# One chain of eight heads in place of two chains of four in the RWKV-7 recurrence of a hybrid layer

## The chip, the cores and the metric

The kernel runs on one core of a Trainium2 chip. The metric is the device time of one execution in microseconds; of several runs the median is given. Below, TensorE is the matmul engine, VectorE, ScalarE and GpSimd are the elementwise engines, SyncE issues most DMA transfers and GpSimd some of the stores. PSUM is the memory into which matmuls write, in eight banks of 512 fp32 columns per partition.

## The reference

One trunk layer over 1152 tokens (1024 latent, 128 context), width 1024, all in fp32. A normalised and modulated input is projected once; four heads of an HGRN2 gated recurrence and eight heads of RWKV-7 time mixing, each in both directions, work on the result; an output projection and a gated ConvFFN follow. The part that the change concerns is RWKV-7:

```python
def rwkv7_scan(r, w, k, v, kk, a, s0):
    ...
    def step(S, inp):
        r_t, w_t, k_t, v_t, kk_t, a_t = inp
        sk = jnp.einsum('bhij,bhj->bhi', S, kk_t)
        S = (S * w_t[:, :, None, :] - sk[..., None] * (kk_t * a_t)[:, :, None, :]
             + v_t[..., None] * k_t[:, :, None, :])
        return S, jnp.einsum('bhij,bhj->bhi', S, r_t)
```

Eight heads of 64 and two directions make sixteen independent states of 64 x 64. The outputs of both directions are added, normalised per head and gated. Context scans start from zero, latent scans from cached states.

## The kernel before, in words

The scan is done in chunks of 64 tokens, 18 chunks (16 of the latents, 2 of the context), in the order `ORDER = [*range(10), 16, 17, *range(10, 16)]`. Forward and backward run side by side: in step n the forward scan takes chunk n and the backward scan chunk 15 - n. A pair p of heads (h = 0, 1 in partitions 0 to 63 and 64 to 127) in direction d is one column block w of 64. Four pairs by two directions are eight blocks; the kernel splits them into two groups g of four blocks, and `chains(0)` and `chains(1)` are two generators that are advanced in turn.

Before the recurrence, `features` works out the decayed operands of each pair and stores them to DRAM: `kr` (L1484) and, from `elim`, the inverted 64 x 64 systems (L1549 to L1565) to `d_ak`, `kb` (L1487, L1489) to `d_kb`, and the values, transposed to tokens by rows, to `d_v` (L1423, one store of 128 columns for each direction and stretch of chunks). One step of one group then does this:

- `load_step` loads `kb` (L1757) and the operand array W, for each h (L1759); `load_values` loads the 64 value rows into half of X (L1766) and copies them into its second slot (L1767). W and X have one buffer for each group.
- `prep`: matmuls of kb and W (L1776), two masked evictions by VectorE for each h (L1781 into W, L1783), four transposes of kb (L1790) and their eviction (L1791).
- R1: eight matmuls of W with X (L1820) into the PSUM tile R, copied to r1 (L1822). R2: eight with r1 (L1827) into R, copied into X for each h (L1829).
- State: L1835 and L1837 into R, multiplied by the chunk's decay into X for each h (L1854). Output: L1846 and L1848 into the PSUM tile Y, copied to yt for each direction (L1872), and stored to `d_y` after every second step (L1875).

Each fp32 matmul shows as two records in the trace. PSUM tiles of the two groups share banks:

```python
plan.tag("r", [(mp, 2048), (mp, 2304)], 256)
plan.tag("y", [(mp, 2560), (mp, 2816)], 256)
```

Bank 4 begins at column 2048 of `mp`, bank 5 at 2560. The tag `a` (banks 2, 3, 6, 7) serves `prep`, the hgrn blocks and the adaLN matmuls.

Other work stands around the recurrence: projections of the HGRN2 inputs (`proj`, L1125 to L1127, matmuls of 128 x 128 by 384 columns), `hgrn_block` with many matmuls of 32 columns (L1646 and others), `hgrn_out`, `ada_block`, and in the end `wo_tile`, the output projection, whose tiles need finished outputs. After that come the ConvFFN (L2120) and its down projection (L2269 to L2271).

The order is not written by hand. Every call is recorded as an operation; a planner (`Plan.schedule`) gives each a cost and simulates the engines, taking at each moment the ready operation with the highest rank: the length of the work that hangs on it, plus a lead for its kind (`LEADS`), plus a nudge for each sixteen operations (`NUDGE`), with penalties for a change of matmul shape on TensorE. Each engine then runs its list in that order. Copies may go to ScalarE or VectorE, stores to SyncE's or GpSimd's queue, as the planner finds them free. Operations inside `plan.together()` stay together.

Of the kernel before, what the change touches and what calls it, by code (L numbers as in the profile page):

```python
# [20 lines left out]
P = 128  # L21
# [25 lines left out]
BUSY = 168.59  # L47
NUDGE = {1: 6, 3: -7, 4: -41, 5: -2, 7: 9, 8: 9, 9: 9, 10: 9, 11: 20, 12: 19, 13: 19, 14: 15, 15: 15, 16: 5, 17: -4, 18: -1, 19: -4, 20: -18, 21: -29, 22: -19, 23: -26, 24: -26, 25: -6, 27: -3, 28: -3, 29: -3, 30: -3, 31: -5, 32: -3, 33: -3, 35: -3, 51: -5, 52: -5, 53: -2, 84: -6, 85: -6, 86: -6, 87: -6, 88: 6, 91: -3, 92: -6, 93: -6, 94: -6, 95: -6, 96: -6, 97: -6, 98: -6, 104: -7, 105: -4, 108: -6, 109: 4, 110: -6, 111: -6, 119: 6, 127: -7, 140: 6, 141: 6, 142: 6, 143: 21, 144: 6, 145: 6, 147: -2, 172: -17, 173: -17, 174: -17, 175: -17, 183: -14, 184: -20, 185: -4, 189: 57, 190: 57, 191: 69, 193: 5, 194: 3, 200: -15, 201: -8, 203: 11, 204: 14, 206: 3, 212: -16, 217: 13, 218: 5, 224: -48, 225: -15, 226: -15, 227: -15, 236: 7, 239: -2, 243: -26, 244: -26, 245: -26, 246: -19, 247: -26, 251: 7, 252: 7, 253: 5, 254: -12, 266: -4, 269: 3, 275: 61, 282: -16, 290: -9, 292: 2, 294: 18, 295: 18, 296: 18, 297: 28, 298: 28, 299: 28, 300: 48, 301: 48, 302: 30, 303: 27, 305: 30, 306: 30, 307: 30, 308: 37, 309: 40, 310: 40, 311: 40, 312: 51, 313: 42, 314: 47, 315: 43, 316: 23, 317: 26, 318: 26, 319: 23, 320: 23, 321: 23, 322: 23, 323: 22, 328: 10, 329: 13, 330: 29, 331: 29, 337: -10, 338: -10, 339: -10, 340: -10, 341: -10, 342: -10, 343: -10, 344: 10, 345: 10, 346: 5, 347: 8, 348: 8, 349: 8, 350: 11, 351: 8, 352: -12, 353: -14, 354: -8, 355: -14, 356: 15, 357: -2, 358: 33, 359: 7, 360: -4, 361: 4, 362: -3, 363: -4, 364: 7, 365: -7, 367: 13, 368: 23, 370: 25, 377: 6, 378: 13, 379: 13, 380: 18, 381: 18, 382: 18, 390: 1, 396: 6, 398: 5, 400: -10, 401: -10, 404: -6, 405: -6, 406: -6, 407: -6, 408: -6, 409: -6, 410: -6, 411: -6, 412: -6, 413: -2, 416: -23, 417: 3, 418: 3, 419: 3, 425: -3, 426: -3, 427: -3, 428: -3, 453: -3, 454: -3, 455: -5, 456: 20, 457: 5, 458: 20, 459: 3, 460: -15, 461: 1, 462: -4, 463: -11, 464: -4, 465: -4, 466: -4, 467: -4, 468: -4, 469: -2, 470: 32, 471: 15, 472: 15, 473: 16, 474: 1, 475: 1, 476: 15, 477: 10, 478: 14, 479: 15, 480: 28, 481: 10, 482: 12, 483: 34, 484: 24, 485: 26, 486: 6, 487: 21, 488: 6, 489: 11, 490: 20, 491: 13, 492: 25, 493: 2, 494: -16, 495: -5, 496: -5, 497: -5, 498: -5, 499: -43, 500: -20, 501: -18, 502: -16, 503: -39, 504: -13, 505: -12, 506: -12, 507: -15, 508: -36, 509: -37, 510: -24, 511: -24, 512: -38, 516: 21, 517: 22, 518: 22, 519: 11, 520: 11, 521: 11, 522: 1, 523: 11, 524: 1, 525: 11, 526: 9, 527: 26, 528: -1, 529: 1, 530: -5, 532: -34, 533: -34, 534: -26, 535: -27, 536: 8, 537: 22, 538: 22, 539: 45, 540: 16, 541: 18, 542: 14, 543: 14, 544: 4, 545: 13, 546: 4, 547: 4, 548: 53, 549: 39, 550: 39, 551: 52}
LEADS = {'ada_block': 46.4, 'bonus_rows': 27.8, 'chains': -35.7, 'const': 113.0, 'conv_rkv': 0.0, 'down_weights': -36.2, 'elim': -4.6, 'features': 0.0, 'ffn_down': 14.5, 'ffn_mid': -1.7, 'finish': 52.5, 'finish_last': -12.3, 'first_columns': -38.6, 'front': 0.0, 'gate_row': 0.0, 'hgrn_block': -3.6, 'hgrn_in': 0.0, 'hgrn_out': 113.5, 'late': -0.7, 'made': 3.5, 'mod_columns': -1.2, 'mod_scale': 70.4, 'modulated': -24.2, 'pair': 8.2, 'param_loads': 9.6, 'params': -96.8, 'post': 3.0, 'prep': 119.5, 'product': -3.4, 'put': 0.0, 'save': 4.8, 'step_kernel': -1.0, 'stored': 0.0, 'three': -10.1, 'total': -0.3, 'turned': 4.0, 'weights': 0.0, 'wo_tile': 5.1}
# [769 lines left out]
def step_kernel(ctx: ExitStack, tc: tile.TileContext, I, O):  # L819
# [52 lines left out]
    def banks(name, first, count, each=1, free=False):  # L872
# [26 lines left out]
    NW = 1  # L899
    Layout(low, 0, N0).add("W", 1536, 2 * NW).add("X", 512, 4).add("ckb", 512, 2).add("ar", 512, 2) \  # L900
        .add("ckt", 512, 2).add("r1", 256, 2).add("amask", 192)
    plan.tag("sv", [(low, 8896), (top, 0)], 256)

    Layout(top, 256, N1).add("yt", 512, 2).add("s_in", 512).add("hs", 2304).add("qyo", 768).add("sco", 384).add("vao", 384).add("g2", 384) \
# [51 lines left out]
    plan.tag("r", [(mp, 2048), (mp, 2304)], 256)  # L956
    plan.tag("y", [(mp, 2560), (mp, 2816)], 256)
# [192 lines left out]
    akr = [[dram(f"d_ak{g}", [P, 16, 4, 192]), dram(f"d_akp{g}", [P, 2, 4, 192])] for g in range(2)]  # L1150
    kbd = [dram(f"d_kb{g}", [P, NCH, 4, P]) for g in range(2)]

    vx = [dram(f"d_v{g}", [T, 512]) for g in range(2)]
# [17 lines left out]
    dcs = cst("dcs", [P, 2, NCH, 4])  # L1171
# [9 lines left out]
    def akr_at(g, n0, n):  # L1181

        return akr[g][0][:, n0:n0 + n] if n0 < 16 else akr[g][1][:, n0 - 16:n0 - 16 + n]
# [189 lines left out]
    def features(p, r, k, v):  # L1373
# [16 lines left out]
        for tb in range(3):  # L1390
# [18 lines left out]
            for d in range(2):  # L1409
# [10 lines left out]
                for ch, n0, n in steps_of(d, 6 * (2 - tb if d else tb), 6):  # L1420
                    at = (ch - 6 * (2 - tb if d else tb)) // 2
                    w0 = P * (2 * (p % 2) + d)
                    st(vx[p // 2][64 * n0:64 * (n0 + n), w0:w0 + P].rearrange("(a p) c -> p a c", p=P),  # L1423
                       vt.rearrange("p (a b) -> p a b", b=P)[:, at:at + n // 2, :])
# [4 lines left out]
            for d in range(2):  # L1429
                sg = tb if d == 0 else 2 - tb  # L1430
                c0 = 6 * sg
                w, g = 2 * (p % 2) + d, p // 2
# [16 lines left out]
                for ch, n0, n in steps_of(d, c0, 6):  # L1449
                    pool.tensor_copy(dcs[:, g, n0:n0 + n, w], dd[:, ch - c0:ch - c0 + n, 64])  # L1450
# [31 lines left out]
                for ch, n0, n in steps_of(d, c0, 6):  # L1482
                    sc_ = slice(ch - c0, ch - c0 + n)
                    st(akr_at(g, n0, n)[:, :, w, 0:128], kr[:, sc_, :])  # L1484

                    ko = kbd[g][:, n0:n0 + n, w, :]
# [8 lines left out]
    def elim(akd, ako, nu, name, tag):  # L1495
# [44 lines left out]
        for c2 in range(2):  # L1540
            for h in range(2):
                for sb in range(2):
# [3 lines left out]
                    if name < NPAIR:  # L1546
                        for d in range(2):
                            u0 = 16 * d + 8 * h
                            o = akr[name // 2][0][hs].rearrange("p (i c) w t -> p i c w t", c=2)  # L1549
                            o = o[:, :, c2, 2 * (name % 2) + d, 128:192]  # L1550
# [6 lines left out]
                    else:  # L1557
                        tv = tt[cs].rearrange("p (g w h) t -> p g w h t", g=2, w=4)
                        for g in range(2):
# [184 lines left out]
    for g in range(2):  # L1744
        for b in range(NW):
            for h in range(2):
                pool.memset(Ws[g][b][hc[1 - h], A0[h]:A0[h] + 768], 0.0)
# [648 lines left out]
```

## Time and profile before

| what | value |
|---|---|
| median of 3 runs | 1820.85 us (1820.06 to 1825.13) |
| profiled execution, time | 1820.69 us |
| profiled execution, span of instructions | 1818.9 us |
| TensorE busy | 1768.3 us, 97% |
| VectorE busy | 1415.1 us, 78% |
| ScalarE busy | 862.0 us, 47% |
| GpSimd busy | 289.3 us, 16% |
| mean granted TensorE clock | 0.993 |

The span reaches from the first to the last instruction; 1.8 us of the time lie outside it. Busy time of an engine counts a stretch once, however many of its instructions overlap, and ends of matmuls are modelled. PE is TensorE, PEld its weight loads, DVE VectorE, ACT ScalarE, POOL GpSimd, SPq the queue of SyncE. L1820 is line 1820 of the kernel. Tiles appear under the name of the memory they lie in (`low`, `top`, `fx`, and `banks` for PSUM), so the recurrence is found by its lines. All of it lies between 482 us and about 972 us.

### The profile page before, as it was taken

How to read it: one execution, taken by the hardware profiler on the slowest of the kernel's cores; microseconds unless marked ns; L12 is line 12 of the kernel's file. 1: busy time of each engine (PE TensorE's matmuls, PEld its weight loads, DVE VectorE, ACT ScalarE, POOL GpSimd, SP SyncE). 2: the span in 40 equal slices, each digit the busy share in tenths (PEclk: the TensorE clock that was granted, in tenths of full speed). 3: DMA queues.
4: the chain of work that ended last, by engine and by line, in shares of the span. 5: the costliest groups of instructions: out<-in, count | busy, mean ns of one | idle time of the engine just before them, and what ended most of it. 6: DMA issues, size and time to landing. Idle time of an engine off the chain costs nothing.

```text
span 1818.9 us, 45180 instructions
## 1 busy us (share of the span) xinstructions
PE 1768.3 (97%) x18402; PEld 1587.1 (87%) x18402; DVE 1415.1 (78%) x2670; ACT 862.0 (47%) x1753; POOL 289.3 (16%) x553
## 2 busy tenths in 40 slices
PE   7999999999999999999999999999999999999998
PEld 5889888899888788888788799999999999888887
DVE  7559899887778888876867889999999954985543
ACT  6556656543255645643636754444444433321321
POOL 2013435353312222122110100000000000000000
PEclk9999999999999999999999999999999999999999
DMA  9325637487757568889967522222222247774451
GB/s 325 102 72 151 147 102 180 128 229 193 207 165 246 165 203 258 267 283 306 324 207 244 203 59 73 73 73 73 73 73 73 76 126 251 227 272 162 133 169 67
DMA packets 272176, 307.45 MB, mean 169 GB/s; under 512 B 62611, under 2 KB 216849, under 8 KB 271968
## 3 DMA queue, kind: packets, MB, share of 16 engines
q1 hardware_dynamic: 245584, 224.33, 41.3%
q0 software_dynamic: 26384, 80.23, 13.1%
q8 instruction: 144, 2.36, 0.5%
q14 instruction: 64, 0.52, 0.1%
HBM read 200.50 MB, written 103.99 MB: 167 GB/s over the span
## 4 chain that ended last, share of the span: by engine, by line
PE 69%; DMA 5%; DVE 3%; ACT 1%; issue 1%; POOL 0%; SPq 0%; DVEq 0%; ACTq 0%; POOLq 0%
PE banks L2120 27%; PE banks L2269 5%; PE banks L2270 5%; PE banks L2271 5%; PE banks L1125 3%; PE banks L1127 3%; PE banks L1126 3%; DMA low<-d_ak 2%; PE banks L2011 2%; PE banks L2013 2%; PE banks L2012 2%; PE banks L1776 1%; PE banks L1827 1%; PE banks L1846 1%; PE banks L1646 1%
## 5 line engine op out<-in xcount | busy, mean ns | idle before, releaser
L1125 PE MATMUL banks<-hh,wh 128*128 128x384 f32 x768 | 282.0, 367 | 0.7 <-DVE fx L1314 0.7
L1127 PE MATMUL banks<-hh,wl 128*128 128x384 f32 x768 | 259.0, 337 | 0.0
L1126 PE MATMUL banks<-hl,wh 128*128 128x384 f32 x768 | 258.7, 337 | 0.0
L2209 DVE SCALAR_TENSOR_TENSOR low<-low,pf 128x1024 f32<-128x1024 f32 x176 | 224.8, 1279 | 4.6 <-ACT low L2203 3.0
L2120 PE MATMUL banks<-qm,wh 128*128 128x320 f32 x968 | 223.3, 310 | 0.0
L2120 PE MATMUL banks<-hbm,wh 128*128 128x256 f32 x880 | 164.4, 283 | 1.3 <-ACT low L1991 1.3
L1125 PEld LDWEIGHTS banks<-hh,wh 128*128 128x128 f32 x768 | 144.9, 189 | 21.0 <-issue 11.4
L2120 PE MATMUL banks<-qm,wl 128*128 128x320 f32 x528 | 162.8, 308 | 0.0
L2120 PEld LDWEIGHTS banks<-qm,wh 128*128 128x128 f32 x968 | 160.7, 189 | 0.1
L1126 PEld LDWEIGHTS banks<-hl,wh 128*128 128x128 f32 x768 | 145.5, 189 | 2.4 <-issue 1.2
L1127 PEld LDWEIGHTS banks<-hh,wl 128*128 128x128 f32 x768 | 145.0, 189 | 0.0
L2120 PEld LDWEIGHTS banks<-hbm,wh 128*128 128x128 f32 x880 | 140.4, 191 | 1.7 <-ACT low L1991 1.7
L2120 PE MATMUL banks<-ham,wh 128*128 128x256 f32 (+1 forms) x616 | 132.4, 295 | 0.0
L2120 PE MATMUL banks<-hbm,wl 128*128 128x256 f32 x440 | 124.8, 284 | 0.0
L2120 PEld LDWEIGHTS banks<-ham,wh 128*128 128x128 f32 x616 | 102.2, 192 | 0.0
L2120 PEld LDWEIGHTS banks<-qm,wl 128*128 128x128 f32 x528 | 99.1, 188 | 0.0
L2269 PE MATMUL banks<-qm,hbm 128*128 128x512 f32 (+1 forms) x240 | 93.7, 390 | 0.0
L2270 PE MATMUL banks<-qm,hbm 128*128 128x512 f32 (+1 forms) x240 | 93.6, 390 | 0.0
L2271 PE MATMUL banks<-qm,hbm 128*128 128x512 f32 (+1 forms) x240 | 93.5, 390 | 0.0
L2090 ACT CAST wh<-fx 128x512 fp32r<-128x512 f32 x88 | 54.3, 620 | 80.6 <-PE banks L2120 76.0
L2158 ACT COPY fx<-banks 128x320 f32<-128x320 f32 (+1 forms) x132 | 52.0, 397 | 84.2 <-PE banks L2120 82.8
L2120 PEld LDWEIGHTS banks<-hbm,wl 128*128 128x128 f32 x440 | 84.4, 192 | 0.0
(527 smaller groups left out, 4333.5 us busy)
## 6 DMA issues: line engine op xcount, KB each, us to landing
wr<-in_w_in_dram SPq DMA_DIRECT2D x34, 512.0 KB, 5.6
d_a<-low POOLq DMA_DIRECT2D x22, 576.0 KB, 3.4
low<-d_ak SPq DMA_DIRECT2D x64, 192.0 KB, 4.4
low<-in_ffn_w_up_dram SPq DMA_DIRECT2D x22, 512.0 KB
wr<-in_ffn_w_gate_dram SPq DMA_DIRECT2D x22, 512.0 KB, 3.7
low<-d_kb SPq DMA_DIRECT2D x36, 256.0 KB, 5.3
low<-d_a SPq DMA_DIRECT2D x12, 704.0 KB, 4.6
low<-in_ada_w_dram SPq DMA_DIRECT2D x32, 256.0 KB, 6.0
```

Source lines behind the costliest of these rows:

```text
L1125: mm(o, wh[:, kt, :], hh[:, kt, c], kt == 0, False)
L1126: mm(o, wh[:, kt, :], hl[:, kt, c], False, False)
L1127: mm(o, wl[:, kt, :], hh[:, kt, c], False, kt == KT - 1)
L2011: mm(ps, oh[:, kt, :], woh, kt == 0, False)
L2012: mm(ps, oh[:, kt, :], wol, False, False)
L2090: split(*w, src)
L2120: pe.matmul(o, a[:, kt, :], b[:, kt, :], start=start and first, stop=last, skip_group_check=not start)
L2158: act.copy(keep[n], y[:, 0:w])
L2209: dve.scalar_tensor_tensor(av, shifted(dy, dx), tap(3 * dy + dx), av, MUL, ADD)
L2269: mm(o, lh, w[:, 0, c], first, False)
L2270: mm(o, lh, w[:, 1, c], False, False)
L2271: mm(o, ll, w[:, 0, c], False, last)
```

## The change

Both groups become one chain of eight blocks.

- `chains` is one generator. W is one array of 2 x 8 x 192 columns, X one of 2 x 8 x 64 for each h. R and Y are tiles of 512 columns, a whole bank each. R1 and R2 are sixteen matmuls each, state and output are twice as long, and r1, X, yt and the multiplied states are evicted in 512 columns at once. `prep` keeps its size and is called twice in a step.
- `d_ak` and `d_kb` are one array each for all eight blocks, so a step has one load of kb and two of W instead of two and four.
- Values: `d_v` is laid out by h, so that one transfer for each h brings 512 contiguous columns; it writes both slots of X (a step of 0 in its source), and the copies of L1767 go. For this `features` stores 64 columns at a time for each h: two stores in place of one.
- `d_y` is stored 512 columns wide, the context part of `elim` stores both groups at once, and `bonus_rows` reads the values by h.
- The order is set anew: `BUSY`, `LEADS` and `NUDGE` have other numbers; the planner is the same.

```diff
-BUSY = 168.59
-NUDGE = {1: 6, 3: -7, 4: -41, ...
-LEADS = {'ada_block': 46.4, 'bonus_rows': 27.8, ...
+BUSY = 173.75
+NUDGE = {1: 6, 3: -7, 4: -41, ...
+LEADS = {'ada_block': 46.4, 'bonus_rows': 15.8, ...
...
-    plan.tag("r", [(mp, 2048), (mp, 2304)], 256)
-    plan.tag("y", [(mp, 2560), (mp, 2816)], 256)
+    banks("r", 4, 1)
+    banks("y", 5, 1)
...
-    vx = [dram(f"d_v{g}", [T, 512]) for g in range(2)]
+    vx = dram("d_v", [T, 2, 8, 64])
...
-                    w0 = P * (2 * (p % 2) + d)
-                    st(vx[p // 2][64 * n0:64 * (n0 + n), w0:w0 + P].rearrange("(a p) c -> p a c", p=P),
-                       vt.rearrange("p (a b) -> p a b", b=P)[:, at:at + n // 2, :])
+                    for h in range(2):
+                        st(vx[64 * n0:64 * (n0 + n), h, 2 * p + d].rearrange("(a p) c -> p a c", p=P),
+                           vt.rearrange("p (a b) -> p a b", b=P)[:, at:at + n // 2, 64 * h:64 * h + 64])
...
+    def load_step(n):
+
+        kb, a = tl("ckb", [P, 8, P]), akr_at(n, 1)
+        ld(kb, kbd[:, n])
         for h in range(2):
-            ld(W[hc[h], A0[h]:A0[h] + 768].rearrange("p (w t) -> p w t", t=192), a[hc[h], 0])
+            ld(W[hc[h], h], a[hc[h], 0])
         return kb
 
-    def load_values(g, n):
+    def load_values(n):
 
         for h in range(2):
-            o = Xs[g][h][hc[1 - h]]
-            ld(o[:, 0], vx[g][64 * n:64 * n + 64].rearrange("t (w h j) -> t w h j", h=2, j=64)[:, :, h])
-            copy(o[:, 1], o[:, 0], ("POOL", "ACT"))
+            v = vx[64 * n:64 * n + 64, h]
+            ld(X[h][hc[1 - h]].rearrange("p a w j -> p a (w j)"), AP(v.tensor, v.offset, [list(v.ap[0]), [0, 2], [1, 512]]))
...
         for j, n in enumerate(ORDER):
-            ar, kt = prep(g, n, kb)
...
+            ops = [prep(g, kb) for g in range(2)]
+            ar = lambda h, w: ops[w // 4][0][:, h, w % 4]
+            kt = lambda h, w: ops[w // 4][1][:, w % 4, hc[h]]
 
             with plan.together():
-                for w in range(4):
-                    for h in range(2):
-                        mm(R[hc[h], 64 * w:64 * w + 64], av(h, w, 0), X[h][:, 0, w], True, True)
-            r1 = tl("r1", [P, 256])
+                for w, h, c in every:
+                    mm(R[hc[h], c], W[:, h, w, 0:64], X[h][:, 0, w], True, True)
+            r1 = tl("r1", [P, 512])
             copy(r1, R)
...
-    cg = [chains(0), chains(1)]
+    steps = chains()
...
     for n in range(NCH + 1):
-        for g in range(2):
-            next(cg[g], None)
+        next(steps, None)
```

More of the change, by code (lines that the diff above doesn't have):

```diff
@@ L1953, in step_kernel @@
                 hgrn_out(a[0])
-    for g in range(2):
-        for _ in cg[g]:
-            pass
+    for _ in steps:
+        pass
     for f, *a in rest:
```

169 lines of the change are left out of this document (77 added, 92 removed).

## The prediction

> **What bounds the kernel now.** I read the page first, then busy time by stage, then the groups of instructions of the recurrence stage, then its timeline. All the merged code runs between 482 us (first prep matmul) and about 972 us; the rest of the kernel is touched only through one store and through the order. Columns of the stage rows: length, then busy us of TensorE, weight loads, VectorE, ScalarE, GpSimd, then granted clock, DMA share, GB/s.
>
> ```profile
> span 1818.9 us, 45180 instructions
> 482.00:965.00 483.00, 463.75 (x8346) 398.54 (x8341) 377.75 (x903) 253.74 (x575) 98.91 (x192) 0.99 0.78 242
> 0.00:482.00 482.00, 463.28 (x4695) 410.34 (x4697) 384.21 (x815) 263.19 (x524) 159.75 (x306) 0.99 0.59 164
> 965.00:1050.00 85.00, 79.11 (x506) 67.03 (x506) 67.57 (x126) 58.83 (x130) 7.62 (x13) 0.97 0.63 214
> 1050.00:1819.00 769.00, 762.21 (x4866) 711.21 (x4865) 585.54 (x828) 286.22 (x527) 22.99 (x42) 0.99 0.37 121
> ```
>
> TensorE is the bound everywhere. In the stage it is busy 463.75 of 483 us, so idle 19.25 us; VectorE is at 78%, ScalarE at 53%. Cheaper evictions on those two therefore pay only where TensorE waits for them, so what matters is what the recurrence costs TensorE. Its groups (mean ns, then idle just before and what ended it):
>
> ```profile
> L1776 PE MATMUL banks<-low 64*128 64x128 f32 x576 | 47.1, 289 | 4.3 <-DMA low<-d_ak 2.5 <-issue 0.8 <-DMA low<-d_akp 0.7
> L1820 PE MATMUL banks<-low 128*64 128x64 f32 x576 | 22.4, 225 | 0.3 <-DVE low L1854 0.3
> L1827 PE MATMUL banks<-low 128*64 128x64 f32 x576 | 24.3, 229 | 3.6 <-issue 1.4 <-ACT low L1822 1.4 <-DVE low L1854 0.3
> L1835 PE MATMUL banks<-low 128*64 128x64 f32 x544 | 34.8, 226 | 0.7 <-DVE low L1854 0.7
> L1846 PE MATMUL banks<-low 128*64 128x64 f32 x576 | 37.0, 227 | 1.2 <-ACT top L1872 1.1
> ```
>
> The matmuls stay the same in number and shape, so the work itself is worth nothing. What changes is how often TensorE enters and leaves it. The timeline shows one visit (start, length, engine, line), then two groups back to back, the pitch inside a run, and the first and last prep:
>
> ```profile
> 488.46 0.33 PE L1125 MATMUL banks<-hh,wh 128*128 128x384 f32 x1
> 488.63 0.33 PE L1126 MATMUL banks<-hl,wh 128*128 128x384 f32 x1
> 488.81 0.34 PE L1127 MATMUL banks<-hh,wl 128*128 128x384 f32 x1
> 489.07 0.69 PE L1820 MATMUL banks<-low 128*64 128x64 f32 x16
> 489.69 0.45 PE L1125 MATMUL banks<-hh,wh 128*128 128x384 f32 x1
> 489.97 0.34 PE L1126 MATMUL banks<-hl,wh 128*128 128x384 f32 x1
> ...
> 819.27 1.15 PE L1820 MATMUL banks<-low 128*64 128x64 f32 x32
> 820.35 0.44 PE L1125 MATMUL banks<-hh,wh 128*128 128x384 f32 x1
> ...
> 971.84 0.29 PE L1846 MATMUL banks<-low 128*64 128x64 f32 x4
> 971.96 0.29 PE L1848 MATMUL banks<-low 128*64 128x64 f32 x4
> ...
> 482.42 0.38 PE L1776 MATMUL banks<-low 64*128 64x128 f32 x2
> 941.73 1.16 PE L1776 MATMUL banks<-low 64*128 64x128 f32 x16
> ```
>
> Dense projection matmuls follow each other every 0.17 us. Going into the recurrence the step is 0.26 (0.09 lost). Four records take 0.12, so 16 take 0.48, yet the visit occupies 0.62 (0.14 lost on leaving), and the second dense matmul comes 0.28 after the first (0.11 lost). One visit between dense work thus loses 0.34 us. Two groups in one visit take 1.08 instead of 2 x 0.62: there joining saves 0.16 us.
>
> **The change part by part.**
>
> *Visits.* Counting unbroken runs of L1820 to L1848 in the timeline gives 102 visits (first at 489.07, last ending with 971.96), those of L1776 give 32: 134. Afterwards 18 steps need at least R1, R2 and state-with-output, 54, and 18 for a joined prep: 72; at most 72 and 36: 108. So 26 to 62 disappear. I take 40, at 0.25 us each, the middle of 0.16 and 0.34: -10 us, with bounds 26 x 0.16 = -4 and 62 x 0.34 = -21. This is on the path, since TensorE is the bound.
>
> *Evictions.* Rows of the nearest shapes:
>
> ```profile
> L1822 ACT COPY low<-banks 128x256 f32<-128x256 f32 x32 | 11.1, 374 | 17.4 <-PE banks L1820 10.1 <-DVE low L1854 3.2 <-PE banks L1880 1.7
> L1829 ACT COPY low<-banks 64x256 f32<-64x256 f32 x58 | 21.2, 366 | 23.0 <-PE banks L1827 13.1 <-DVE low L1829 6.1 <-PE banks L1837 1.1
> L1829 DVE COPY low<-banks 64x256 f32<-64x256 f32 x14 | 5.9, 422 | 8.1 <-PE banks L1827 5.7 <-ACT low L1829 2.3
> L1791 ACT COPY low<-banks 128x512 f32<-128x512 f32 x31 | 18.0, 586 | 19.6 <-PE banks L1790 19.4
> L1791 DVE COPY low<-banks 128x512 f32<-128x512 f32 x5 | 3.5, 692 | 2.4 <-PE banks L1790 2.2
> L1854 DVE TENSOR_TENSOR low<-banks,dcs 64x256 f32<-64x256 f32 x60 | 25.0, 420 | 10.8 <-PE banks L1837 6.9 <-PE banks L1820 1.8 <-ACT low L1822 1.1
> L1767 POOL COPY low<-low 64x256 f32<-64x256 f32 x33 | 15.8, 478 | 94.4 <-DMA low<-d_v 74.0 <-PE banks L1776 10.1 <-PE banks L1835 8.0
> L1767 ACT COPY low<-low 64x256 f32<-64x256 f32 x35 | 14.0, 402 | 40.5 <-DMA low<-d_v 40.1
> L1781 DVE TENSOR_TENSOR low<-banks,low 64x256 f32<-64x256 f32 x72 | 30.4, 422 | 14.6 <-PE banks L1776 13.1
> ```
>
> Partitions do not count (366 against 374 ns), columns do: two copies of 256 columns on ScalarE, 0.73 to 0.75 us, become one of 512 at 0.59; on VectorE 0.84 become 0.69. Each step loses some 0.6 us of eviction plus the four L1767 copies, which also leave ScalarE and GpSimd standing 40.1 and 74.0 us in their queues behind d_v loads. All this lies beside TensorE: I cost it at nothing. If TensorE waited for ScalarE it would be a gain, so it cannot hurt.
>
> *The shared bank.* Both groups' R lie in one bank, both Y in another, and accesses to it already go one after the other:
>
> ```profile
> 491.21 0.42 DVE L1829 COPY low<-banks 64x256 f32<-64x256 f32 x1 [0.78 <-PE banks L1827]
> 491.67 0.37 ACT L1829 COPY low<-banks 64x256 f32<-64x256 f32 x1 [1.49 <-DVE low L1829]
> ```
>
> The second half of the same eviction waits for the first although it reads other partitions. So the two chains were less independent than they look: a group's matmuls wait for the other's evictions. L1846 behind L1872 (1.1 us) and L1835 behind L1854 (0.7) are such waits; they go: -2 us. Taking none of them as cross waits gives 0.
>
> *The step's load.* W is single in both kernels; its load starts after the last Y. Until now the other group could run meanwhile; now all eight heads wait, and with them prep, masks and R1. Behind the W loads on SyncE stand the loads of the other work (gates, state stacks, adaLN weights). On the chain of waits (start, length, what) the load already shows:
>
> ```profile
> 493.73 8.04 DMA low<-d_ak
> 528.63 6.18 DMA low<-d_ak
> ```
>
> TensorE hides it behind projections, hgrn blocks and adaLN matmuls; what it did not hide is 2.5 + 0.7 us at L1776 over 36 loads. If each of the 18 steps pays 0.4 us, the mean of the six waits behind 2.5 us, that is 7.2 against 3.2 now: +4 us. Bounds: -3 (half the loads, all hidden) and, uncovered, 18 x 6.2 = +112, to which 0.4 is far nearer because the cover stays. SyncE issues half as many loads; values go twice from DRAM instead of being copied, as hidden as before.
>
> *The v store.* In the features stage each store of 128 columns becomes two of 64, pieces of 256 instead of 512 bytes:
>
> ```profile
> L1423 POOL DMA_DIRECT2D d_v<-top x22: 567/760/785, 123.6 to 369.5; - x22
> q1 hardware_dynamic: 245584, 224.33, 41.3%
> 200.00:400.00 200.00, 194.32 (x2485) 171.14 (x2486) 177.88 (x366) 118.88 (x245) 90.42 (x163) 0.99 0.65 166
> 800.00:900.00 100.00, 97.55 (x1638) 82.84 (x1631) 68.97 (x163) 46.00 (x98) 19.81 (x38) 1.00 1.00 313
> ```
>
> 32 more issues by 0.76 us are 24 us of queue, on a GpSimd busy 159.75 of 482 us: nothing, and 24 us spread over 250 if that cover were gone. q1 spends 41.3% of 16 x 1819 us on 245584 packets, 49 ns each. The stores come to 1152 rows x 4 pairs x 2 directions = 9216 packets; as many again cost 28 us of all 16 DMA engines: the share rises from 0.65 to 0.76, still below the 1.00 of 800 to 900 us, where TensorE stays 97.5% busy. Nothing.
> [...]
>
> *Order elsewhere.* Outside the stage the same operations stand in another order; TensorE's idle time there is 18.7 + 5.9 + 6.8 us. I take 0, with bounds of 4 us either way: the granted clock of 0.97 over 85 us is 2.5 us, and such dips may move.
>
> Sum against the profiled execution, 1820.69 us (span 1818.9 and 1.8 around it; the median of the runs is 1820.85): -10 - 2 + 4 = -8, so **1813 us**.
>
> **The rivals.**
>
> *The single chain becomes the bound (slower).* One step costs: load 7.1 (mean of the two pieces), prep 2 x 1.09 and two masks of 0.42, so 3.0; R1 1.08; copy 0.59; R2 1.08; two serial copies 1.28; 128 records of state and output matmuls at 0.12 for four, 3.8; three hand-overs of 0.3. Together 18.7 us against 483/18 = 26.8 per step. With two groups, one's waits covered the other's. Now each of five returns to the chain waits on TensorE's in-order queue behind filler. It decides from 8.1 us of such waits per step on, 1.6 us per return; each further microsecond costs 18 us. One over: 1821 - 10 + 18 = 1829 us; two: 1847. For it: d_ak loads and VectorE at 78%. Against it: filler in plenty, the slack of 8.1 us.
>
> *No net gain.* Longer bursts need longer filler, and filler is cut into as many pieces as before: the visits of 32-column work take the place of those saved. 1820 us, within 4.
>
> [...]
>
> **How the numbers follow.** Chances: forecast 0.52, chain as bound 0.32, no net gain 0.12, small packets 0.04. A change of 0.3%, 5.5 us, is about what a measurement of this kernel can tell from none (its three runs lie 0.28% apart). The forecast's own range is 1801 (visits -16, order -4) to 1818. Of its 0.52, 0.46 lie below 1815.3; 0.06 lie within, with no net gain and 0.03 of small packets: 0.21. Slower: 0.32 and 0.01. The range goes to 1834, which takes in half of the chain rival; below 1801 little is left.
>
> **What would show it.** Right: unbroken runs of recurrence matmuls fall from 134 to about 94; TensorE's idle in the stage stays near 19 us; copies of 512 columns take 0.59 and 0.69 us; the stage is shorter by 6 to 10 us, the others unchanged. Wrong: idle time before L1776 or R1 grows beyond 10 us; the last step ends much after 972 us with output-projection work left waiting; visits stay above 120; or the difference lies before 482 or after 1050 us.

## The result and the profile after

The changed kernel takes 1841.5 us (median of 4 runs, 1831.9 to 1845.3), the kernel before beside it 1820.5. The ratio is 1.010, with a 95% interval of 1.006 to 1.014: slower by some 20 us, where 8 us less was forecast. The profiled execution took 1842.7 us (span 1840.9).

In the new listing preparation is L1767 (it was L1776), R1 L1807, R2 L1813, state L1822 and L1824, output L1833 and L1835; the loads are L1749 (kb), L1751 (W), L1758 (X). First the head of the page and the same stretches as in the prediction (length, then busy us of TensorE, weight loads, VectorE, ScalarE, GpSimd, then clock, DMA share, GB/s):

```profile
span 1840.9 us, 44633 instructions
0.00:482.00 482.00, 455.60 (x4577) 402.93 (x4578) 376.70 (x799) 265.30 (x533) 160.65 (x306) 0.99 0.60 162
482.00:965.00 483.00, 448.96 (x8346) 390.71 (x8345) 357.23 (x832) 209.81 (x437) 69.33 (x129) 0.99 0.81 244
965.00:1050.00 85.00, 83.79 (x533) 69.06 (x532) 66.24 (x125) 49.73 (x110) 9.47 (x18) 1.00 0.71 243
1050.00:1841.00 791.00, 776.66 (x4952) 723.70 (x4950) 607.37 (x868) 299.59 (x557) 24.02 (x44) 0.99 0.37 121
```

TensorE idles 34.0 us in the stage of 483 us, where it idled 19.3. The clock of the rows is the same to two digits. The bounds of the merged code stand in the source lines' answers (count, duration min/median/max, first and last start):

```profile
L1767 PE MATMUL banks<-low x576: 267/272/559, 489.7 to 969.3; 64*128 64x128 f32 x192
L1835 PE MATMUL banks<-low x576: 221/222/271, 508.4 to 991.1; 128*64 128x64 f32 x192
L2106 PE MATMUL banks<-qm,wh x968: 304/310/417, 1054.0 to 1554.1; 128*128 128x320 f32 x194
```

```profile
L2120 PE MATMUL banks<-qm,wh x968: 305/310/392, 1033.8 to 1531.6; 128*128 128x320 f32 x194
```

The second fence is the kernel before, whose first preparation was at 482.4. So the loss of 22.0 us of span between the two profiles divides into three: 7.3 ahead of the first preparation, 12.9 from there to the first ConvFFN matmul (551.4 us before, 564.3 after), 1.8 behind it. The groups of the recurrence, and then two of TensorE's waits (who waited, for whom: us in all, times, longest):

```profile
L1767 PE MATMUL banks<-low 64*128 64x128 f32 x576 | 45.9, 289 | 3.5 <-DMA low<-d_ak 2.2 <-issue 0.8 <-DMA low<-d_akp 0.4
L1807 PE MATMUL banks<-low 128*64 128x64 f32 x576 | 21.9, 230 | 2.3 <-DMA low<-d_v 2.3
L1822 PE MATMUL banks<-low 128*64 128x64 f32 x544 | 35.7, 230 | 2.2 <-issue 2.2
L1824 PE MATMUL banks<-low,c_ident 128*64 128x64 f32 x544 | 35.5, 228 | 3.5 <-issue 3.5
L1833 PE MATMUL banks<-low 128*64 128x64 f32 x576 | 36.1, 225 | 0.7 <-issue 0.7
```

```profile
PE banks L1459 <- DVE top L1450: 8.5, 3, 7.1
PE banks L1643 <- issue: 6.8, 4, 3.1
```

Waits for nothing that the profile shows ("issue") have grown: at L1822, L1824 and L1643 there were none of this size. The longest stands in the middle of one unbroken run of 24 records (timeline of TensorE; in the brackets, the idle time before and what ended it):

```profile
733.25 0.33 PE L1643 MATMUL banks<-top 128*32 128x32 f32 x14
736.71 0.29 PE L1643 MATMUL banks<-top 128*32 128x32 f32 x10 [3.13 <-issue]
```

No operand that the profile shows ended this wait, after the fourteenth record of the run. The page lists a DMA queue that the prediction never looked at:

```profile
q8 instruction: 144, 2.36, 0.5%
```

These are 144 packets of 16384 bytes. If each brings 256 instructions, that makes 36864, close to the 36804 records of TensorE's matmuls and weight loads. Lining up the packets with these records, TensorE's semaphore instructions counted among them, shows where TensorE waits for them, in both traces (all counted from 0): record 256k + 449 never starts less than 1.1 us after the end of packet k (at the least 1.28 us in the changed kernel, 1.09 before), while record 256k + 448 starts up to 1.9 us ahead of that end in the changed kernel. Where the packet is late, TensorE stands still until 1.1 to 1.7 us after its end (a starved gap below). Which record asks for a packet is not shown; record 256k + 128 is taken for the request, an estimate: in both traces no packet starts less than 1.0 us after it. At the gap above this record was issued at 727.3, the packet began at 733.9 and ended at 735.3, and TensorE went on at 736.7. Before has 5 such gaps (3.5 us in all), after 19 (22.5 us). In the stage they make 17.5 of the 34.0 us that TensorE idles, against 2.2 of 19.3 before: about the whole growth. The time from request to packet has a median of 3.5 us in the stage before and 4.1 us after.

Stretches of half clock come after the longest gaps (the clock is the third number from the right):

```profile
577.70:581.10 3.40, 3.40 (x58) 2.94 (x47) 2.33 (x5) 1.66 (x3) 0.00 (x0) 0.50 0.93 313
605.00:608.40 3.40, 3.40 (x63) 3.39 (x63) 1.72 (x6) 0.15 (x1) 0.00 (x0) 0.50 0.57 146
738.10:741.50 3.40, 3.40 (x44) 3.11 (x44) 2.27 (x7) 0.53 (x1) 0.49 (x1) 0.51 1.03 266
```

They begin 0.2, 0.1 and 1.4 us after the ends of the three longest starved gaps, at 577.5, 604.9 and 736.7 us. A fourth stretch of 3.4 us, from 782.5, begins within a wait of R1 for d_v (2.3 us, to 783.1). Over all runs the mean granted clock is 0.989 for the change and 0.994 for the kernel before (17 runs). Span times the missing share is 19.8 and 10.5 us, so up to 9 us of the difference, an estimate, lies in the clock. The kernel before has one such stretch in its stage too, of 6.8 us from 501.6, with no long gap ahead of it; so the link is read from the timing, not tested.

That gave three theories. A: the merged runs (128 records of state, 128 of output) outrun the instruction supply. B: the step's loads are at fault, by delaying the instruction packets. C: the loss is a wait for data on the single chain, and the gaps are by the way. B and C both put it on the loads. The newly set order elsewhere is a fourth candidate (experiment 6).

### The profile page after: what moved, and what is told of

Its sections match the earlier page's. It is cut to its first block, busy times and chain, and to the rows that moved or that the text cites. A ratio compares the mean times of both kernels' runs of the same rounds, so it can differ in the third digit from the quotient of the medians.

```text
span 1840.9 us, 44633 instructions
## 1 busy us (share of the span) xinstructions
PE 1765.0 (96%) x18402; PEld 1586.4 (86%) x18402; DVE 1407.5 (76%) x2623; ACT 824.4 (45%) x1635; POOL 263.5 (14%) x495
## 4 chain that ended last, share of the span: by engine, by line
PE 83%; DMA 7%; DVE 4%; issue 4%; ACT 1%; POOL 1%; SPq 0%; DVEq 0%; POOLq 0%; ACTq 0%
PE banks L2106 27%; PE banks L1123 7%; PE banks L1125 6%; PE banks L1124 6%; PE banks L2255 5%; PE banks L2256 5%; PE banks L2257 5%; DMA low<-d_ak 2%; PE banks L1767 1%; PE banks L1997 1%; PE banks L1999 1%; PE banks L1998 1%; DMA wr<-d_o 1%; PE banks L1643 1%; PE banks L1361 1%
## 5 line engine op out<-in xcount | busy, mean ns | idle before, releaser
L2144 ACT COPY fx<-banks 128x256 f32<-128x256 f32 (+1 forms) x132 | 52.2, 397 | 86.5 <-PE banks L2106 86.5
L2255 PE MATMUL banks<-qm,hbm 128*128 128x512 f32 (+1 forms) x221 | 86.4, 391 | 0.0
L2256 PE MATMUL banks<-qm,hbm 128*128 128x512 f32 (+1 forms) x221 | 86.4, 391 | 0.0
L2257 PE MATMUL banks<-qm,hbm 128*128 128x512 f32 (+1 forms) x221 | 86.3, 390 | 0.0
```

The source lines that it names most:

```text
L2144: act.copy(keep[n], y[:, 0:w])
L2255: mm(o, lh, w[:, 0, c], first, False)
L2256: mm(o, lh, w[:, 1, c], False, False)
L2257: mm(o, ll, w[:, 0, c], False, last)
```

## The experiments

All variants keep the planner's order of their kernel: the edit is made when instructions are issued, after the order is set, so nothing else moves. It is shown below as if made in the source, shortened. Times are medians; ratios are to the kernel before, run beside them.

### 1. Fewer records for the same work

```diff
 with plan.together():
+    for h in range(2):
+        mm(R[hc[h], 0:512], ident[:, hc[h]], X[h][:, 0, 0:8], True, False)
     for w in range(8):
         for h in range(2):
-            mm(R[hc[h], c], kt(h, w), X[h][:, 1, w], True, False)
-        for h in range(2):
-            mm(R[hc[h], c], ident[:, hc[h]], X[h][:, 0, w], False, True)
+            mm(R[hc[h], c], kt(h, w), X[h][:, 1, w], False, w == 7)
```

> The changed kernel in its own order, with one edit at the moment of issue: the old state is added into R (L1824) by two identity matmuls of 512 columns ahead of the k-transposed ones, in place of sixteen of 64 columns behind them. The sum, the columns streamed and every other instruction stay; some 56 of TensorE's records a step (17 steps) go, and the unbroken run of R3 and Y falls from 256 records to 200. Theory A (TensorE runs out of instructions: after its 256-record runs it stands still until the next 16384-byte packet of its instruction queue has landed, 19 gaps of 22.5 us in all in the trace of after against 5 of 3.5 us in before): the gaps fall to about half, and the time by 8 to 15 us, to 1827-1834. Theory B (the fetch is slow only because the step's loads are in its way): gaps shrink little, time within 4 us of 1841. Theory C (the loss is a wait for data on the single chain, and the gaps are by the way): no change within 3 us, since nothing on the chain is shorter.

> The same edit in the kernel before: per group of four heads two identity matmuls of 256 columns in place of eight of 64. Its runs of R3 and Y fall from 128 records to 104. Theory A: before hardly runs out of instructions (3.5 us in all), so it gains at most 3 us: 1817-1821. If each small matmul simply cost time of its own, it would gain about as much as the changed kernel does (8 us and more), and theory A would be wrong on why.

The changed kernel: 1838.2 us (1.008, 1.006 to 1.010). The kernel before: 1821.5 (0.999, 0.998 to 1.001), as theory A has it. In the changed kernel the gaps shrank as theory A has it, from 22.5 to 9.7 us, but the time by 3 us only, not 8 to 15, and the intervals do not tell that from nothing. Waits for loads grew, and the clock in the stage of this profile is 0.97:

```profile
L1767 PE MATMUL banks<-low 64*128 64x128 f32 x576 | 46.1, 291 | 6.3 <-DMA low<-d_ak 4.3 <-ACT top L1640 1.0 <-DVE low L1772 0.6
L1822 PE MATMUL banks<-low 128*64 128x64 f32 x544 | 19.7, 227 | 0.0
L1824 PE MATMUL banks<-low,c_ident 128*64 128x512 f32 x68 | 19.1, 641 | 0.0
482.00:965.00 483.00, 452.02 (x7833) 382.05 (x7833) 358.08 (x837) 211.26 (x440) 71.45 (x132) 0.97 0.81 247
```

The "issue" at both state lines is gone; the wait for d_ak went from 2.2 to 4.3 us. Theory A explains the gaps and not the time; how much of the missing gain went into the clock and how much into the waits is not shown.

### 2. The loads taken away

```diff
-ld(W[hc[h], h], a[hc[h], 0])
+ld(W[hc[h], h, 0:1, 0:64], a[hc[h], 0, 0:1, 0:64])    # X likewise
```

This holds from the second step on. The edit reached W and X; kb stayed whole, against what the first expectation says. The matmuls run on stale data.

> The changed kernel in its own order; from the second step of the recurrence on, the loads of kb, W and X (about 1.8 MB a step) bring only 256-byte slivers, so most of what the matmuls read is stale: this part of the computation is left out. TensorE's instructions are all there. Theory B (the loads hold up the instruction packets): the time from request to packet falls from a median of 4.0 us to under 3 us in the recurrence, the starved gaps from 22.5 us to under 8, and with the 4 us of waits for loads the time falls by 15 to 20 us, to 1822-1826. Theory A with the length of the runs as the whole cause: the gaps stay above 15 us, and the time falls by 4 to 8 us, to 1833-1837.

> The kernel before in its own order, its loads of W and X cut to 256-byte slivers from the second step on, as in the light version of the changed kernel (whose edit reached W and X, 1.3 MB a step, while kb, 0.5 MB, stayed whole); most of what the matmuls read is stale, so this part of the computation is left out. The light version of the changed kernel took 1808.4 us, 33 less than with its loads. If the loads cost the merged chain more than the two chains (theory B): this one falls by 15 us or less, to 1805-1815, and with light loads the merged kernel is the equal of the other or better. If the loads cost both the same, and the loss lies elsewhere (order, runs): it falls by 30 us or more, to about 1790, and the merged kernel stays some 20 us behind.

The changed kernel falls to 1808.4 us (0.992, 0.990 to 0.994), the kernel before to 1809.0 (0.992, 0.990 to 0.995). Without these loads the whole difference of 20 us is gone. The loads cost the merged chain 33 us, more than any theory had expected, and the two chains 13. So the loads are the cause of the total, as B and C have it. The starved gaps fall to 7.3 us, the median request to packet to 2.8 us, and the stage rows compare as follows (changed kernel, then before, both with light loads):

```profile
482.00:965.00 483.00, 470.71 (x8567) 409.11 (x8565) 378.80 (x876) 224.10 (x466) 73.20 (x136) 1.00 0.66 217
L2106 PE MATMUL banks<-qm,wh x968: 304/310/468, 1018.2 to 1519.4; 128*128 128x320 f32 x194
```

```profile
482.00:965.00 483.00, 467.45 (x8519) 402.60 (x8518) 382.63 (x910) 259.82 (x590) 100.86 (x194) 1.00 0.66 215
L2120 PE MATMUL banks<-qm,wh x968: 305/310/392, 1024.6 to 1521.6; 128*128 128x320 f32 x194
```

First preparation to first ConvFFN matmul is 531.9 us in the merged kernel (from 486.3) and 540.7 in the other (from 483.9): 8.8 us shorter. This is about the gain that the prediction counted on; 2.4 us ahead of the stage and 3.5 behind it eat most of it.

The preparation with light loads, in the changed kernel and in the one before:

```profile
L1767 PE MATMUL banks<-low 64*128 64x128 f32 x576 | 41.5, 284 | 1.3 <-DVE low L1772 1.3
L1776 PE MATMUL banks<-low 64*128 64x128 f32 x576 | 41.2, 284 | 0.0
```

Busy and idle together are 42.8 and 41.2 us here, against 49.4 and 51.4 with the loads whole. So the loads cost the preparation 6.6 us in the changed kernel and 10.2 us in the kernel before: its wait did not grow by the change, it fell. What grew lies elsewhere. An estimate of the 20 us by which the loads cost the merged chain more, from these profiles and all runs' clocks: starved gaps +16 (light loads take 15 from the changed kernel and none from the other, 3.5 to 4.3), the clock up to +6 (19.8 to 11.7 us, against 10.5 to 8.6), R1 behind d_v +2, the preparation -4. The terms can overlap.

### 3. The instruction supply by itself

```python
for n in (128, 256, 384, 512, 2048):
    for j in range(n // 4):    # second version; the first has h = 0:64 throughout
        h, c = (slice(64 * x, 64 * x + 64) for x in (j % 2, j // 2 % 8))
        mm(small[h, c], raw[:, h], raw[:, c], True, True)
    dense(100)
```

> A kernel that computes none of the reference and only measures the instruction supply: runs of 128, 256, 384, 512 and 2048 records of the recurrence's small matmul (128 by 64 fp32, 64 columns), with 100 matmuls of 512 columns between runs; three stages: no loads, loads in 2048-byte pieces all along, loads in 24576-byte pieces all along. Theory A: in the quiet stage the run of 128 goes at the full 68 records per us, the runs of 384 and 512 show gaps, and the run of 2048 settles at 35 to 50 records per us, set by the packets. Theory B: the quiet stage shows no gap up to 512 records and the loaded ones do; the long run is at least 1.5 times as slow beside loads as in the quiet stage. If the long run keeps 68 records per us in all stages, both theories fall.

> The first measuring kernel gave its small matmuls all to one half of TensorE's columns and ran at 34 records per us, at which it never ran out of instructions; request to packet took 1.5 us in its quiet stage and 4.3 to 6.7 us beside loads. Here the matmuls alternate between the two halves, as in the recurrence; nothing of the reference is computed. Theory A: 68 records per us in the quiet stage for runs of 128 and 256, gaps from 384 on, and a long run limited to 45 to 60 records per us by a packet of 256 records every 4 to 5.5 us. Theory B: the quiet stage keeps 60 or more even in the long run; beside loads, with 5.5 us and more from request to packet, runs of 384 and over show gaps and the long run falls to 30 to 40 records per us. Both can hold in part: the gap of the loaded stage over the quiet one is the share of theory B.

The first version ran at 34 records per us (9984 in 294.4 us of busy time), at which nothing starved. The second alternates between output partitions 0 to 63 and 64 to 127 as the recurrence does. Its windows: a run of 384 records in the quiet stage, the same beside loads, and the run of 2048 in the quiet stage.

```profile
146.60:152.40 5.80, 5.80 (x193) 5.66 (x192) 0.00 (x0) 0.00 (x0) 0.00 (x0) 1.00 0.01 3
379.20:387.10 7.90, 5.89 (x193) 5.75 (x192) 0.00 (x0) 0.00 (x0) 0.00 (x0) 1.00 1.01 428
205.80:235.80 30.00, 30.00 (x1025) 29.92 (x1024) 0.00 (x0) 0.00 (x0) 0.00 (x0) 1.00 0.02 4
```

```profile
379.21 5.11 PE L89 MATMUL small<-raw 128*64 128x64 f32 x167
386.33 0.92 PE L89 MATMUL small<-raw 128*64 128x64 f32 x25 [2.01 <-issue]
```

In quiet, 2048 records in a row go at 68.3 per us (2049 in the window of 30.0 us) without a gap: request to packet is mostly 1.1 to 2.3 us there. Beside 428 GB/s of loads it is 3.7 to 7.2 us, in pieces of 2048 as of 24576 bytes, and one of the runs of 384 or 512 in each loaded stage stops, for 2.0 and 1.5 us. (The loads had ended before the long runs of those stages, so the limit of a long run beside loads was not measured.) So theory A's plain form is wrong: no run of up to 2048 records starves TensorE by itself. Long runs only make it exposed to a fetch that the loads have slowed.

### 4. X written once

One part of the change is undone in the changed kernel, and the same part alone is made in the kernel before.

```diff
-ld(X[h][hc[1 - h]], AP(v.tensor, v.offset, [.., [0, 2], [1, 512]]))
+ld(X[h][hc[1 - h], 0], AP(v.tensor, v.offset, [.., [1, 512]]))
+pool.tensor_copy(X[h][hc[1 - h], 1], X[h][hc[1 - h], 0])
```

```diff
-copy(o[:, 1], o[:, 0], ("POOL", "ACT"))
+ld(o[:, 1], vx[g][..][:, :, h])
```

> The changed kernel in its own order with one part of the change undone: X's values are loaded into one slot and copied to the second by GpSimd (as the kernel before does at L1767), in place of being written by the DMA twice; 0.26 MB of 1.83 MB of loads a step go. If the bytes loaded in the recurrence set the loss in proportion (33 us for 1.3 MB in the light version): 5 to 8 us less, 1833-1836. If the loss hangs on when the loads start and on the latency of the first bytes: within 3 us of 1841. If the copies on GpSimd hold up its stores: some us more.

> One part of the change alone, in the kernel before and in its own order: X's values are written to both slots by the DMA (two loads of 256-byte pieces per group and h) in place of one load and the copy at L1767; 0.26 MB a step more. By the light versions, before loses 13 us to 1.06 MB a step and the changed kernel 33 us to 1.3 MB, so the same dose should cost before about 3 us (1823-1827), where undoing it in the changed kernel gave 10. If the double write costs by its bytes whatever the chain: about 10 us, 1829-1834. If the copies of ACT and GpSimd were worth more than the bytes: faster than 1821.

> Both edits of the changed kernel: X written once and copied, and the old state added by two matmuls of 512 columns a step. The wide matmuls alone gave 3 us (1838.2, gaps in which TensorE waits for instructions 22.5 us to 9.7 us). If the two costs are separate they add: 1829-1833. If both act through the late instruction packets, the second finds little left: 1834-1838.

X once: 1831.3 us (1.005, 1.003 to 1.007), 10 less where 5 to 8 were expected. The double write alone in the kernel before: 1843.7 (1.010, 1.008 to 1.013), 20 more, not the 3 expected; it loads in pieces of 256 bytes there, so 18432 more packets (18 steps, 2 groups, 2 h, 64 rows, 4 pieces), where the changed kernel has 2304 more of 2048. This one line costs the kernel before as much as the whole change did. It costs without starving: its gaps are 4.7 us in all. Its mean clock is 0.991, against 0.993 in the kernel before beside it, and its waits are for data (preparation of that kernel):

```profile
L1776 PE MATMUL banks<-low 64*128 64x128 f32 x576 | 48.2, 293 | 9.8 <-DMA low<-d_ak 7.5 <-DMA low<-d_akp 1.6 <-DVE top L1736 0.5
```

Before, that wait was 2.5 us. In the changed kernel the wait of R1 for d_v (2.3 us) goes with the second write. The hardware queue's rows (packets, MB, share of 16 engines), after and with X once:

```profile
q1 hardware_dynamic: 237964, 230.13, 43.0%
```

```profile
q1 hardware_dynamic: 235660, 225.41, 41.5%
```

That is 791.6 against 759.6 us of all engines, 32 us for 2304 packets fewer. The packets' own time is about half of it: those of 2048 bytes take 0.114 us each between 482 and 1000 us, so 2304 of them make 16 us of all engines; the rest is other packets that take longer (those of 2048 bytes 0.103 with X once). With the wide matmuls too: 1825.8 us (1.001, 0.999 to 1.003). They are worth 5.5 us here; the two edits add up, and to a little more than expected.

### 5. W in halves

In place of two loads of eight windows, four of four windows, windows 0 to 3 of both h first.

```diff
-for h in range(2):
-    ld(W[hc[h], h], a[hc[h], 0])
+for q in range(2):
+    for h in range(2):
+        ld(W[hc[h], h, 4 * q:4 * q + 4], a[hc[h], 0, 4 * q:4 * q + 4])
```

> The changed kernel with one edit alone: the two loads of W in four halves, windows 0 to 3 first (X is written twice by the DMA, and the old state is added by narrow matmuls, as in the change). If the exposed load of the merged step is a cost of its own, beside the double write of X: some 8 us below 1841, 1831-1835, as on the version with both other edits. If it pays only once the double write is gone, since the queue is what holds the second half: 1838 or more.

> The changed kernel with X written once and the wide matmuls (1825.8 us), and its two loads of W cut into four, first both loads of windows 0 to 3, then those of 4 to 7, so that the first half of the step's preparation can start on half of W, as in the kernel before. If the exposed load of the merged step (the prediction's +4) still costs: 2 to 5 us less, 1821-1824. If the preparation waits for kb or X instead, or the queue's extra issues cost as much: within 2 us of 1826.

> The kernel before with each group's two loads of W in four halves of two windows, in the same manner. Its first group of four windows is prepared in one go, which needs all of its W, so a half that lands earlier starts nothing: within 3 us of 1822. If smaller loads in themselves spread better over the DMA engines (that, not the earlier start of the preparation, gave the 9 us): 4 to 9 us less, 1813-1818.

> The version of the changed kernel with X once, wide matmuls and W in halves (1817.0 us), with W in eight loads of two windows each. If what pays is that the preparation of windows 0 to 3 starts on its own half: nothing more, 1815-1819, or 1 to 3 us more for eight issues on SyncE's queue. If smaller loads in themselves are better: 3 us and more below, 1808-1814.

> The version of 1817.0 us without its wide matmuls: X written once and W in halves, the old state added by sixteen narrow matmuls a step as in the change. If TensorE's instruction supply is a cost of its own even when the loads are mended (theory A in its weaker form): its starved gaps are 5 us or more above those of the version with wide matmuls (6.7 us), and the time is 3 to 7 us above, 1820-1824. If the late instruction packets were only another face of the loads: within 2 us of 1817.

| version | us | ratio to before, 95% |
|---|---|---|
| change + halves | 1826.5 | 1.002 (1.000 to 1.003) |
| change + X once + halves | 1820.2 | 0.998 (0.996 to 0.999) |
| change + X once + wide + halves | 1817.0 | 0.996 (0.995 to 0.998) |
| the last with quarters | 1825.9 | 1.002 (1.000 to 1.004) |
| before + halves of its loads | 1828.7 | 1.003 (1.002 to 1.005) |

Halves alone give 15 us, where 8 were expected. Smaller loads do not pay everywhere: the kernel before, whose groups need all of their load at once, gets slower by 6, and quarters lose 9 again, both more than expected. That work can start on the first half is one reading of this, and it is not shown. The pieces that a load is made of change too. W comes in pieces of 6144 bytes in the change, of 3072 with halves and in the kernel before, of 1536 with quarters and in the halved loads of the kernel before. So all these runs also fit a rival that no run tests: that pieces of 3072 bytes suit this stage best. In the traces a piece of 6144 bytes takes 0.40 us of its DMA engine, one of 3072 0.17, one of 1536 0.08. And with halves alone the preparation starts 0.9 to 3.6 us after the last piece of W has ended in 10 of the 17 steps that follow the first; there the early start cannot be what pays.

By the rows, the preparation accounts for some 5 of the 15 us (49.4 to 44.3), and the starved gaps fall by 9, from 22.5 to 13.4 us. The preparation with halves alone:

```profile
L1767 PE MATMUL banks<-low 64*128 64x128 f32 x576 | 41.9, 284 | 2.4 <-issue 1.7 <-DVE low L1772 0.7
```

The best version, whose preparation without halves takes 46.3 us, with 6.4 idle:

```profile
L1767 PE MATMUL banks<-low 64*128 64x128 f32 x576 | 46.3, 290 | 6.4 <-DMA low<-d_ak 3.3 <-DVE top L1705 1.2 <-DMA low<-d_akp 0.8
```

```profile
L1767 PE MATMUL banks<-low 64*128 64x128 f32 x576 | 42.6, 284 | 2.1 <-DVE low L1772 1.7 <-DMA low<-d_ak 0.4
L2106 PE MATMUL banks<-qm,wh x968: 304/310/468, 1025.5 to 1526.2; 128*128 128x320 f32 x194
482.00:965.00 483.00, 465.61 (x8051) 393.60 (x8050) 376.01 (x863) 221.06 (x459) 99.76 (x170) 0.99 0.78 245
```

L1767 is busy 3.7 us less and idle 4.3 us less: nearly half of the gain is not in the listed idle time. Records overlap (one lasts 0.27 us, a run of 16 takes 1.16), so a wait between two records of a run is listed only from the end of the first, and the rest counts as busy. TensorE's idle time in the stage is 17.4 us, less than before the change. This version beats both kernels. Taking the wide matmuls out of it costs 3 us (gaps of 11.7 us against 6.7), as the weaker form of theory A expected; the two intervals overlap.

### 6. The order ahead of the recurrence

Six d_ak stores and a load of wr were moved behind the d_kb stores that a buffer of `features` waits for, in the version of 1825.8 us.

```diff
-st d_ak (L1554) x6 ... ld wr (L1291) ... st d_kb (L1487) x3
+st d_kb (L1487) x3 ... st d_ak (L1554) x6 ... ld wr (L1291)
```

> The changed kernel with X written once and the wide matmuls (1825.8 us), and six d_ak stores and one load of wr in front of the recurrence moved behind the d_kb stores that a kb buffer of the features waits for (TensorE L1459 waited 5.9 us in all for VectorE L1450, itself behind this buffer). If that is what the newly set order costs ahead of the recurrence: the wait falls below 3 us and the time by 2 to 5 us, to 1821-1824. If other stores or the DMA's own time hold the buffer: within 2 us of 1826.

A miss: 1831.7 us (1.005, 1.003 to 1.007), and the wait grew.

```profile
PE banks L1459 <- DVE top L1450: 9.2, 2, 8.6
```

The wait is there in every profile of the changed kernel (4.7 to 9.2 us), and 0.4 us in the same stretch of every profile of the kernel before (L1461 behind L1452). That it comes from the new order is argued, not shown; what would remove it stays open.

## Why the prediction was wrong, step by step

*Visits (-10): the count right, the price not contradicted.* Unbroken runs fell from 134 to 100 (94 forecast), by a count in the timeline, and with light loads the stretch up to the ConvFFN is 8.8 us shorter than that of the kernel before under the same cut. That holds all that the change does there, the shared bank too; no run prices the visits alone.

*Evictions: right in size, and worth nothing, as said.* 64 partitions by 512 columns, on ScalarE and on VectorE:

```profile
L1815 ACT COPY low<-banks 64x512 f32<-64x512 f32 x26 | 15.1, 580 | 12.7 <-PE banks L1813 7.7 <-DVE low L1815 4.7
L1859 DVE COPY top<-banks 64x512 f32<-64x512 f32 x15 | 10.3, 686 | 14.3 <-PE banks L1835 12.9 <-ACT top L1859 1.4
```

0.58 us on ScalarE and 0.69 on VectorE (0.59 and 0.69 forecast). ScalarE and GpSimd are busy 44 and 30 us less in the stage, for nothing in return. But the step counted the copies that go as a saving of idle engines, when they had spared the queue a second load.

*The step's load (+4, bounds -3 and +112): the step that failed.* Taking the loads of W and X away gives 33 us in the changed kernel and 13 before, so the merged loads cost 20 us more, not 4. The term has two parts. "As hidden as before" was said of the values that go twice from DRAM: undoing that gives 10 us. And the exposed load was priced by the mean of the waits that the profile lists in front of L1776 (0.4 us); cutting W in halves gives 15 us by itself. Why 0.4 was too little: it looked for the price at the preparation alone. There the listed idle time (4.3 us) understates the wait (10.2 us by the light run), but this wait fell by the change, to 6.6. The price is paid in other places, above all in late instruction packets (gaps of 22.5 us against 3.5) and, by the estimate above, in the half clock, which the prediction's sum has no term for. The two prices overlap: both edits give 21 us together with wide matmuls left out (1841.5 to 1820.2).

*The shared bank (-2).* L1846 behind L1872 and L1835 behind L1854 are gone from the rows. R1 behind d_v (2.3) and the "issue" at L1822 and L1824 (5.7) stand in their place.

*The v store: nothing, right.* Between 200 and 400 us the DMA share is 0.64, not the 0.76 expected. The 32 more stores are there (64 at L1421), but a packet of 256 bytes takes 0.020 us between 100 and 482 us and one of 512 bytes 0.031, where the prediction took the mean of all packets, 0.049. The chances count 0.04 for small packets, each dearer for being small; no run shows that: two of 256 bytes take longer than one of 512 (0.040 against 0.031 us), but each takes less.

*Order elsewhere (0, within 4): some 5 us in place of 0, outside the bounds.* The first preparation starts at 484.5 to 489.7 us in ten profiles of the changed kernel and its variants, at 481.6 to 485.9 in five of the kernel before: 3 us on the mean, not the 7.3 of the one profile. Behind the stage it is 2 to 3 us.

*The rivals.* The single chain did become dearer, by the time and on the side that the rival named (1829 to 1847). Its mechanism is not borne out: the waits at the preparation fell, and most of the new idle time is starved gaps, which it does not name. With light loads the merged stage is the shorter one, so the rest of the chain does not bound it; but the load is 7.1 of the rival's 18.7 us a step (its terms add up to 18.8), so this run does not test the chain as a whole. Of the marks set for "right", TensorE's idle time in the stage failed (34 us, not 19). Of those for "wrong", two came true: the last step ended at 991, not 972, and part of the difference lay before 482 us. The idle time before L1767 stayed at 3.5 us, so that mark looked in the wrong place. The forecast's lower end of 1801 counts visits and order alone; with its +4 and -2 it would be 1803.

What stays open: of the 20 us, halves give 15, X once 10, wide matmuls 3 to 5, which overlap and together give 24.5. How much of each works through late instructions, through late data and through the clock is not told apart, since an edit that removes one lets the other come forward. Whether halves pay by the earlier start or by their pieces of 3072 bytes is open too.

## What to carry to other kernels

A copy that an engine makes in its idle time can be cheaper than a transfer that "lies beside the work" (by 10 us in the changed kernel and 20 in the one before, experiment 4): price bytes in the stage where they fall, at that stage's DMA share (0.78 here). When two interleaved chains are merged, try the merged load in its old pieces, in the order in which they are used; here that paid 15 us, whichever of the two did it. Listed idle time understates waits for data (4.3 us where light loads show 10.2); compare the busy time of the waiting line with that of undisturbed runs. And a load can be paid for where nothing waits for its data: look at the instruction queue (here 22.5 us of starved gaps against 3.5) and the clock (0.989 against 0.994).

## What the runs showed of the hardware

- TensorE's instructions come by DMA: 144 packets of 16384 bytes for 36804 records of matmuls and weight loads, so 256 to a packet. A packet takes a median of 1.06 us on its engine, in the changed kernel as before. Record 256k + 449 starts at the least 1.28 us after the end of packet k in the changed kernel, 1.09 us before.
- Counted from record 256k + 128, the estimate of the request, a packet starts mostly 1.1 to 2.3 us later in quiet and 3.7 to 7.2 us later beside 428 GB/s of loads (second version of experiment 3). The quiet run of 2048 records has no gap; the changed kernel has gaps of 22.5 us.
- Small fp32 matmuls that alternate between output partitions 0 to 63 and 64 to 127 go at 68.3 records per us (2049 in 30.0 us); all to partitions 0 to 63, at 34 (9984 in 294.4 us).
- In the stage of the changed kernel, 3.4 us of half clock follow each of the three starved gaps in which TensorE idled more than 2 us (2.2 to 3.1 us). A fourth such stretch begins within a wait of 2.3 us for data.
- More and smaller loads of the same bytes cost time in two runs: halves in the kernel before 6 us, quarters in the best version 9 us. By what is not shown.
